# A hybrid decoder block on one core: sums of weight blocks by accumulating DMAs in the GLA value and gate projections

## The chip, the cores and the metric

The kernel runs on one core of one Trainium2 chip. The metric is the device time of one execution in microseconds. Before the change the median of three runs is 1661.94 us (1661.82 to 1663.04).

## The reference

One layer of a decoder block over 256 tokens of width 2048, float32 throughout. What matters here is the input projection and the two of its parts that the change touches, v and the output gate of the gated linear attention (GLA):

```python
proj = x @ w_in                      # x: (256, 2048), w_in: (2048, 13336)
gq, gk, gv, gr, glr, fq, fk, fv, ff, ma, mb = split(proj)
v = gv.reshape(B, S, 4, 512)         # gv: 2048 columns
o = gla_chunked(q, k, v, log_a)      # chunked linear attention, per-head RMS norm
o = o * silu(gr)                     # gr: 2048 columns, the output gate
y_gla = o @ w_branch_gla
# FoX attention -> y_fox; merged = sigmoid(ma)*y_gla + sigmoid(mb)*y_fox; merged @ w_out;
# layer norm; conv-gated MLP; layer norm; x + sigmoid(x W_g) * (p W_p)
```

## The kernel before

All weights are streamed once from DRAM, cut into units of 128 x 2048 floats that are numbered in the order of their use (`wu[u]`). A unit arrives as two tiles of 128 x 1024 (`raw`, a ring of five buffers) by DMAs on SyncE's queue, whose order is written out by hand. Each tile is split into a high part, which ScalarE rounds to the fast matmul format (`copy`, L112), and a low part, which VectorE gets as the difference (L220, L194); a product is then the three matmuls high x high, high x low, low x high. The rings `hi` and `lo` hold six tiles each. `unit(ahead=3)` prepares units up to two ahead of the one that TensorE uses. On the other engines a scheduler fixes the order of instructions when the program is built, and each engine then works in that order.

GLA's v (units 52 to 67) and gate (68 to 83) are computed in halves of 1024 output columns. The two halves of v and the first half of the gate are made by `s_half`: eight units a half, each holding one pair of 128-row blocks of the inner dimension. For a classic pair TensorE runs 24 matmuls of 512 columns. For a pair in the set `GV_S` or `GR_S` it uses a seven-product form of the 2 x 2 block product (Strassen's, in Winograd's arrangement), 21 matmuls: three of its weight operands are blocks as loaded (x11, x21, x22) and four are combinations of the four blocks b11, b12, b21, b22 of 128 x 512 (t1, t2, t3, t4). The combinations of the activations (`xS`) are made once per pair by `x_sums`. After the last seven-product pair of a half, `fold` adds the seven products up (L819), and `ev_v`, `ev_r0` (L913, L927) evacuate the half. The gate's second half is made by `x_half`, with classic units alone.

`prep_s` prepares a seven-product unit. Before, VectorE makes four differences in place in the raw tiles (`differences`, L148), two on the first tile and two on the second:

```python
if h == 0:
    sub(b11, b12, b11)
    sub(b12, b12, b22)
else:
    sub(b22, b22, b11)
    sub(b21, b21, b22)
```

The same function prepares the units of the output projection and of the down projection (u >= 120), which partly come with combinations that were parked in DRAM earlier. Seven-product units before: 53, 55, 57 (v, half 0), 61, 63, 65 (v, half 1), 69, 71 (gate, half 0).

Of the kernel before, what the change touches and what calls it, by code (L numbers as in the profile page):

```python
# [14 lines left out]
ALU = mybir.AluOpType  # L15
# [32 lines left out]
WO_ORDER = (tuple(range(8)), tuple(range(8)))  # L48
OUT_ORDER = (tuple(range(8)), (0, 1, 3, 2, 5, 4, 6, 7))
GV_S = ((1, 3, 5), (1, 3, 5))  # L50
GR_S = ((1, 3), ())
X_S = (1, 3, 5)
WO_S = ((1, 3, 5), (1, 3, 5))
WO_C = (0, 2, 4, 6, 7)
# [18 lines left out]
def tile_block(ctx: ExitStack, tc: tile.TileContext, wu, wfv, wpp, xT_in, x_in, pT_in, wlr,  # L73
               chan, gnorm, lng, ident_in, mask_in, cmask_in, out):
    nc = tc.nc
# [45 lines left out]
    for _ in range(8):  # L121
# [6 lines left out]
    s_units = {b + nh * len(order[nh]) + i  # L128
               for b, order, sset in ((52, WO_ORDER, GV_S), (68, WO_ORDER, GR_S),
                                      (120, OUT_ORDER, WO_S), (dn0, DN_ORDER, DN_S))  # L130
               for nh in range(2) for i, n in enumerate(order[nh]) if n in sset[nh]}
    ready = {}
# [34 lines left out]
    def prep_s(u):  # L167


        r0, r1 = [ring.tile([P, 1024], F32, tag="raw", bufs=5, name=f"raw{u}_{h}")  # L170
                  for h in range(2)]
        b12, b11, b22, b21 = r0[:, 0:512], r0[:, 512:1024], r1[:, 0:512], r1[:, 512:1024]
        rt = (r0, r1)
        if u in parked:
            nc.sync.dma_start(b11, wu[u, :, 512:1024])
            nc.sync.dma_start(r1, wu[u, :, 1024:2048])
            w = s8([P, 2048], name=f"td{u}")
            nc.sync.dma_start(w, td[parked[u]])
            rt = (w[:, 0:1024], w[:, 1024:2048])
        else:  # L180
            for h, r in enumerate((r0, r1)):
                nc.sync.dma_start(r, wu[u, :, h * 1024:(h + 1) * 1024])
        if dn0 <= u < dn0 + NF:
            nh = (u - dn0) // (NF // 2)
            pair = DN_ORDER[nh][(u - dn0) % (NF // 2)]
            hS[nh, pair] = s8([P, 4, 256], F32R, name=f"hS{nh}_{pair}")
            nc.sync.dma_start(hS[nh, pair].bitcast(F32), sd[DN_S[0].index(pair)].rearrange(
                "p (i n) -> p i n", i=4))

        def split(src, name, e=slice(0, 1024)):  # L190
            hi = rhi.tile([P, 1024], F32R, tag="hi", name=f"hi{u}_{name}")[:, e]
            lo = lo_tile(u, f"{u}_{name}")[:, e]
            copy(hi, src)
            nc.vector.tensor_tensor(lo, src, hi.bitcast(F32), ALU.subtract)  # L194
            return [(hi[:, o:o + 512], lo[:, o:o + 512]) for o in range(0, src.shape[1], 512)]

        x11, = split(b11, "b11", slice(512, 1024))
        x22, x21 = split(r1, "b2")
        if u not in parked:
            differences(r0, r1, 0)  # L200
        t3, t1_ = split(rt[0], "t13")
        if u not in parked:
            differences(r0, r1, 1)
        t2_, t4 = split(rt[1], "t24")
        ready[u] = [x11, x21, x22, t1_, t3, t2_, t4]
# [232 lines left out]
    for u in range(8):  # L438
        hi, lo = fvu[u]
        for j in range(2):  # L440
            kt = 2 * u + j
            a = xT[kt // 4][:, kt % 4, :]
# [6 lines left out]
            for t, i, c in seq:  # L449
                o, n = fch[c]  # L450
                w, x = prods[t][i]
# [288 lines left out]

        return o[:, i, 0:P], o[:, i, P:256]

    def s_sums(y):

        a11, a21, a12, a22 = [y[:, k, t * P:t * P + P] for k in range(2) for t in range(2)]
        v = t2("sums").rearrange("p (i t) -> p i t", t=P)
        for i, a, b, op in ((0, a21, a22, ALU.add), (2, a21, a11, ALU.subtract),
                            (1, v[:, 0], a11, ALU.subtract), (3, a12, v[:, 1], ALU.subtract)):
            nc.vector.tensor_tensor(v[:, i], a, b, op)
        return v  # L750

# [18 lines left out]
    def s_half(nm, nh, order, sset, cl, st, zof, ev, tail=0, mid={}, end=None, ahead=3,  # L770
               residual=True):

        if nh == 0:
            C = [[mmtile(f"{nm}0_{t}{c}") for c in range(2)] for t in range(2)]
            p1, p5 = [mmtile(f"{nm}0_p{i}") for i in (1, 5)]
            p6, p7 = [mxtile(f"{nm}0_p{i}") for i in (6, 7)]
        else:  # L780
            C = [[f(f"{nm}1_{t}{c}") for c in range(2)] for t, f in enumerate((mxtile, mmtile))]
            p1, p5, p6, p7 = [mmtile(f"{nm}1_p{i}") for i in (1, 5, 6, 7)]
        prods = (p1, C[0][0], C[0][1], p5, p7, p6, C[1][0])
        left = (0, 1, 6, 3, 5, 4, 2)
        n, ns = len(order), len(sset)
        todo = {id(C[t][c]): 6 * (n - ns) for t in range(2) for c in range(2)}
        for p in prods:
            todo[id(p)] = todo.get(id(p), 0) + 3 * ns
        total = dict(todo)

        def mm(ps, x, w):
            nc.tensor.matmul(ps, lhsT=x, rhs=w, start=todo[id(ps)] == total[id(ps)],  # L792
                             stop=todo[id(ps)] == 1)
            todo[id(ps)] -= 1

        def classic(pair, w, toks=(0, 1), cs=(0, 1)):
            for j in range(2):
                for t in toks:
                    ah, al = cl(pair, j, t)
                    for x, v in ((ah, w[0][j]), (ah, w[1][j]), (al, w[0][j])):  # L800
                        for c in cs:
                            mm(C[t][c], x, v[:, c * 512:c * 512 + 512])

        def strassen(pair, ops):
            for ps, i, (hi, lo) in zip(prods, left, ops):
                ah, al = st(pair, i)
                for x, v in ((ah, hi), (ah, lo), (al, hi)):
                    mm(ps, x, v)

        def fold():  # L810
            g0, g1 = 2 * nh, 2 * nh + 1
            u = t2("fold")
            axpy = lambda z, p: nc.vector.scalar_tensor_tensor(z, z, ALPHA, p, ALU.mult, ALU.add)
            add = lambda z, p: nc.vector.tensor_tensor(z, z, p, ALU.add)
            if not residual:
                copy(zof(0, g0), p1)
                for o, x, p in ((u, zof(0, g0), p6), (zof(0, g1), u, p5), (zof(1, g0), u, p7),
                                (zof(1, g1), zof(1, g0), p5)):
                    nc.vector.tensor_tensor(o, x, p, ALU.add)  # L819
                return  # L820
            copy(u, p1)
            axpy(zof(0, g0), p1)
            add(u, p6)
            axpy(zof(0, g1), u)
            add(zof(0, g1), p5)
            add(u, p7)
            axpy(zof(1, g0), u)
            add(u, p5)
            axpy(zof(1, g1), u)

        for i, pair in enumerate(order[:n - tail]):
            (strassen if pair in sset else classic)(pair, unit())
            if i in mid:
                mid[i]()
            if pair in sset and not set(order[i + 1:]) & set(sset):
                fold()
        us = [unit(ahead) for _ in range(tail)]

        def tail_mm(t, c, i):
            classic(order[n - tail + i], us[i], (t,), (c,))  # L840
            if i == tail - 1:
                ev(t, c, C[t][c])

        if tail:
            end(tail_mm)
            return
        for t in range(2):
            for c in range(2):
                ev(t, c, C[t][c])
# [4 lines left out]
    def x_sums():  # L854
        o = s8([P, 8, 256], F32R, name="xS")
        for i, pair in enumerate(X_S):
            if i < 2:
                xS[pair] = [o[:, 4 * i + j, :] for j in range(4)]
            else:
                w = [sm.tile([P, 512], F32R, tag="t2", bufs=6, name=f"xS{i}{j}") for j in range(2)]  # L860
                xS[pair] = [w[j // 2][:, j % 2 * 256:j % 2 * 256 + 256] for j in range(4)]
            y = t2("xy").rearrange("p (k t) -> p k t", t=S)
            nc.sync.dma_start(y, xT_in[:, 2 * pair:2 * pair + 2, :])
            v = s_sums(y)
            for j in range(4):
                hi = xS[pair][j][:, 0:P]
                copy(hi, v[:, j])
                nc.vector.tensor_tensor(xS[pair][j][:, P:256], v[:, j], hi.bitcast(F32),
                                        ALU.subtract)
            yield  # L870
# [53 lines left out]
    def ev_r0(t, c, ps):  # L924
        z = vg[c][:, 1, t, :]
        with tc.high_priority(P_STAT):
            nc.vector.tensor_tensor(z, z, ps, ALU.add)  # L927
        gate(z, z)

    s_half("gr", 0, WO_ORDER[0], GR_S[0], x_cl, x_st, lambda t, g: vg[g][:, 1, t, :], ev_r0,  # L930
           residual=False)
# [76 lines left out]
    for n in range(16):  # L1008
# [27 lines left out]
        i = WO_C.index(pair)  # L1036
# [242 lines left out]
    for n in range(NF):  # L1279
# [9 lines left out]
        y = t1("yc")  # L1289
# [8 lines left out]
        u = t1("up")  # L1298
# [14 lines left out]
        if pair in DN_S[0] and j == 1:  # L1313
            v = s_sums(yp)
# [199 lines left out]
def _layout(i):  # L1514
# [4 lines left out]
    for n in range(16):  # L1519
        br.append(bg[n:n + 1])  # L1520
        if n % 2 == 0:
# [5 lines left out]
        [np.stack([_wst(c("fq", 1024)), _wst(c("fk", 1024))], 1).reshape(16, P, 2048), qk.reshape(16, P, 2048), m[:PSM1],  # L1527
         _sst(c("gv", 2048), WO_ORDER, GV_S), _sst(c("gr", 2048), WO_ORDER, GR_S), m[PSM1:]] + br
        + [_sst(i["w_out"][0], OUT_ORDER, WO_S), gu,
# [45 lines left out]
```

## Time and profile before

| | |
|---|---|
| median of 3 runs | 1661.94 us (1661.82 to 1663.04) |
| span of the profiled execution, its own time | 1661.1 us |
| TensorE (PE) matmuls | 1655.3 us busy |
| VectorE (DVE) | 1278.4 us busy |
| ScalarE (ACT) | 887.5 us busy |
| GpSimd (POOL) | 61.3 us busy |
| granted TensorE clock | 1.00 |
| v and gate half 0 | 371.3 to 496.5 us of the span |

The profile records one execution, from its first to its last instruction; the runs' times also hold the little that lies around it. Matmuls are pipelined, so the length of one is more than the distance to the next. In the rows "a<-b" stands for the tile written and the tiles read, and "[0.88 <-ACT hi L112]" for idle time of the engine just before an instruction and what ended it.

### The profile page before, as it was taken

How to read it: one execution, taken by the hardware profiler on the slowest of the kernel's cores; microseconds unless marked ns; L12 is line 12 of the kernel's file. 1: busy time of each engine (PE TensorE's matmuls, PEld its weight loads, DVE VectorE, ACT ScalarE, POOL GpSimd, SP SyncE). 2: the span in 40 equal slices, each digit the busy share in tenths (PEclk: the TensorE clock that was granted, in tenths of full speed). 3: DMA queues.
4: the chain of work that ended last, by engine and by line, in shares of the span. 5: the costliest groups of instructions: out<-in, count | busy, mean ns of one | idle time of the engine just before them, and what ended most of it. 6: DMA issues, size and time to landing. Idle time of an engine off the chain costs nothing.

```text
span 1661.1 us, 24309 instructions
## 1 busy us (share of the span) xinstructions
PE 1655.3 (100%) x8935; PEld 1438.3 (87%) x8935; DVE 1278.4 (77%) x1927; ACT 887.5 (53%) x1297; POOL 61.3 (4%) x204
## 2 busy tenths in 40 slices
PE   9999999999999999999999999999999999999999
PEld 9988888888888888888898888888888888888887
DVE  7666877888876757888987777877777787898774
ACT  6655555555554654455575455555555555556543
POOL 0100000000000000000010010000000000000000
PEclk9999999999999999999999999999999999999999
DMA  8745455546564557878856587777777668798554
GB/s 321 251 164 172 169 176 171 188 158 199 196 232 172 174 181 275 309 244 301 315 171 206 207 291 266 251 243 249 254 249 255 204 226 322 275 364 316 178 188 158
DMA packets 101959, 383.74 MB, mean 231 GB/s; under 512 B 11544, under 2 KB 12832, under 8 KB 95696
## 3 DMA queue, kind: packets, MB, share of 16 engines
q1 hardware_dynamic: 97584, 359.11, 62.1%
q0 software_dynamic: 4256, 23.08, 3.7%
q8 instruction: 70, 1.15, 0.3%
q14 instruction: 49, 0.40, 0.1%
HBM read 358.02 MB, written 24.13 MB: 230 GB/s over the span
## 4 chain that ended last, share of the span: by engine, by line
PE 98%; DMA 0%; DVE 0%; ACT 0%; POOL 0%; SPq 0%; issue 0%; POOLq 0%
PE dn L792 11%; PE psu L287 9%; PE psg L287 9%; PE psm L287 7%; PE pg L333 5%; PE psu L289 5%; PE psg L289 5%; PE gv L792 4%; PE wo L792 4%; PE psm L289 4%; PE psa L287 4%; PE dn_p L792 3%; PE gr L333 3%; PE fv L452 2%; PE gr L792 2%; PE psa L289 2%
## 5 line engine op out<-in xcount | busy, mean ns | idle before, releaser
L220 DVE TENSOR_TENSOR lo<-raw,hi 128x1024 fp32r<-128x1024 f32 x502 | 611.0, 1223 | 240.4 <-ACT hi L112 238.7
L112 ACT ACTIVATE hi<-raw 128x1024 fp32r<-128x1024 f32 x502 | 528.4, 1058 | 430.5 <-issue 169.2
L287 PE MATMUL psu<-x1T,hi 128*128 128x512 f32 x688 | 240.4, 392 | 0.0
L287 PE MATMUL psg<-x1T,hi 128*128 128x512 f32 x672 | 234.8, 392 | 0.0
L289 PE MATMUL psu<-x1T,lo 128*128 128x256 f32 x688 | 192.4, 280 | 0.0
L289 PE MATMUL psg<-x1T,lo 128*128 128x256 f32 x672 | 187.9, 280 | 0.0
L287 PE MATMUL psm<-xT,hi 128*128 128x512 f32 x512 | 181.2, 396 | 0.0
L287 PEld LDWEIGHTS psu<-x1T,hi 128*128 128x128 f32 x688 | 129.2, 188 | 27.6
L287 PEld LDWEIGHTS psg<-x1T,hi 128*128 128x128 f32 x672 | 126.2, 188 | 26.9
L289 PE MATMUL psm<-xT,lo 128*128 128x256 f32 x512 | 143.2, 280 | 0.0
L289 PEld LDWEIGHTS psu<-x1T,lo 128*128 128x128 f32 x688 | 130.7, 190 | 0.0
L289 PEld LDWEIGHTS psg<-x1T,lo 128*128 128x128 f32 x672 | 127.6, 190 | 0.0
L287 PEld LDWEIGHTS psm<-xT,hi 128*128 128x128 f32 x512 | 96.2, 188 | 19.7
L792 PE MATMUL dn<-hi,hC 128*128 128x512 f32 x400 | 111.3, 389 | 0.0
L289 PEld LDWEIGHTS psm<-xT,lo 128*128 128x128 f32 x512 | 97.2, 190 | 0.1
L287 PE MATMUL psa<-oT,hi 128*128 128x512 f32 x256 | 89.5, 392 | 0.0
L792 PEld LDWEIGHTS dn<-hi,hC 128*128 128x128 f32 x400 | 75.0, 188 | 15.6
L112 ACT ACTIVATE hi_t<-raw 128x1024 fp32r<-128x1024 f32 x40 | 42.5, 1063 | 66.0 <-DVE raw L148 51.5
L112 ACT ACTIVATE hi_b<-raw 128x512 fp32r<-128x512 f32 x66 | 55.4, 842 | 40.9 <-DMA raw<-in_wu_dram 15.2
L289 PE MATMUL psa<-oT,lo 128*128 128x256 f32 x256 | 71.6, 280 | 0.0
L194 DVE TENSOR_TENSOR lo_b<-raw,hi_b 128x512 fp32r<-128x512 f32 x66 | 62.5, 954 | 9.9 <-ACT hi_b L112 9.9
L333 PE MATMUL pg<-hi,x2T 128*128 128x512 f32 (+1 forms) x256 | 69.7, 380 | 0.0
(372 smaller groups left out, 3126.3 us busy)
## 6 DMA issues: line engine op xcount, KB each, us to landing
raw<-in_wu_dram SPq DMA_DIRECT2D x555, 512.0 KB, 4.9
td<-in_wu_dram SPq DMA_DIRECT2D x13, 1024.0 KB, 8.4
td<-td POOLq DMA_DIRECT2D x13, 1024.0 KB, 6.9
td<-td SPq DMA_DIRECT2D x13, 1024.0 KB, 7.5
hS<-sd SPq DMA_DIRECT2D x19, 512.0 KB, 7.6
fvraw<-in_wfv_dram SPq DMA_DIRECT2D x13, 524.0 KB, 6.9
sd<-hs POOLq DMA_DIRECT2D x20, 256.0 KB, 5.4
lnb<-in_lng_dram SPq DMA_DIRECT2D x4, 1024.0 KB, 9.8
```

The source lines that it names most:

```text
L112: return nc.scalar.activation(o, i, AF.Copy, bias=0.0, scale=scale)
L194: nc.vector.tensor_tensor(lo, src, hi.bitcast(F32), ALU.subtract)
L220: i = nc.vector.tensor_tensor(lo, raw, hi.bitcast(F32), ALU.subtract)
L287: nc.tensor.matmul(ps, lhsT=hi[i // 8 if hoff == 0 else 0][:, w0 % 1024:w0 % 1024 + P], rhs=a[:, kt % 4, :], start=first and i == 0, stop= ...
L289: nc.tensor.matmul(ps[:, 256:512], lhsT=lo[i // 8 if hoff == 0 else 0][:, w0 % 1024:w0 % 1024 + P], rhs=a[:, kt % 4, 0:256], start=False, ...
L333: nc.tensor.matmul(bs[j][:, 0:m], lhsT=x, rhs=v[:, o:o + m], start=first and i == 0, stop=last and i == 2)
L452: nc.tensor.matmul(fbk[t][c][:, 0:n], lhsT=x, rhs=w[:, o:o + n], start=kt == 0 and i == 0, stop=kt == 15 and i == 2)
L792: nc.tensor.matmul(ps, lhsT=x, rhs=w, start=todo[id(ps)] == total[id(ps)], stop=todo[id(ps)] == 1)
```

## The change

For all units below 84 that are prepared by `prep_s`, the seven-product form is replaced by one with other signs, in which the four weight combinations are sums only: b12 + b11, (b12 + b11) + b22, b22 + b12, b21 + (b11 + b12 + b22). Two of the four (the first and the third) are made by DMAs that add a block from DRAM to a block that is already in SBUF; these are issued by GpSimd (`nc.gpsimd.dma_start(..., accum_op=ALU.add)`), 256 KB each. The other two are VectorE additions. The tiles split afterwards hold (t1, t2) and (t3, t4) instead of (t3, t1) and (t2, t4), and TensorE still takes the operands in the order x11, x21, x22, t1, t3, t2, t4. The activation sums get the matching signs in `x_sums`, the folds of these halves likewise. Pair 5 of the gate's first half (unit 73) becomes a seven-product pair. In the program's order on GpSimd the first DMAs of units 55, 63 and 71 stand ahead of the second DMAs of units 53, 61 and 69. The order of the other instructions on VectorE and ScalarE stays, except around unit 73, whose splits come before the gate's fold.

```diff
-GR_S = ((1, 3), ())
+GR_S = ((1, 3, 5), ())
@@ prep_s
+        if u < 84:
+            b12d, b11d = wu[u, :, 0:512], wu[u, :, 512:1024]
+            nc.gpsimd.dma_start(b12, b11d, accum_op=ALU.add)
+            x11, = split(b11, "b11", slice(512, 1024))
+            x22, x21 = split(r1, "b2")
+            nc.vector.tensor_tensor(b11, b12, b22, ALU.add)
+            nc.gpsimd.dma_start(b22, b12d, accum_op=ALU.add)
+            t1_, t2_ = split(r0, "t12")
+            nc.vector.tensor_tensor(b21, b21, b11, ALU.add)
+            t3, t4 = split(r1, "t34")
+            ready[u] = [x11, x21, x22, t1_, t3, t2_, t4]
+            return
@@ s_sums
-    def s_sums(y):
+    def s_sums(y, plus=False):
...
-        for i, a, b, op in ((0, a21, a22, ALU.add), (2, a21, a11, ALU.subtract),
-                            (1, v[:, 0], a11, ALU.subtract), (3, a12, v[:, 1], ALU.subtract)):
+        for i, a, b, op in (((0, a21, a22, ALU.subtract), (2, a11, a21, ALU.subtract),
+                             (1, v[:, 0], a11, ALU.subtract), (3, a12, v[:, 1], ALU.add))
+                            if plus else
+                            ((0, a21, a22, ALU.add), (2, a21, a11, ALU.subtract),
+                             (1, v[:, 0], a11, ALU.subtract), (3, a12, v[:, 1], ALU.subtract))):
@@ fold, not residual
-                for o, x, p in ((u, zof(0, g0), p6), (zof(0, g1), u, p5), (zof(1, g0), u, p7),
-                                (zof(1, g1), zof(1, g0), p5)):
-                    nc.vector.tensor_tensor(o, x, p, ALU.add)
+                for o, x, p, op in ((u, p6, zof(0, g0), ALU.add), (zof(0, g1), p5, u, ALU.subtract),
+                                    (zof(1, g0), p7, u, ALU.add),
+                                    (zof(1, g1), p5, zof(1, g0), ALU.subtract)):
+                    nc.vector.tensor_tensor(o, x, p, op)
@@ x_sums
-            v = s_sums(y)
+            v = s_sums(y, True)
```

## The prediction

> **What bounds the kernel now.** I read the page first: busy times and the chain that ended last.
>
> ```profile
> span 1661.1 us, 24309 instructions
> PE 1655.3 (100%) x8935; PEld 1438.3 (87%) x8935; DVE 1278.4 (77%) x1927; ACT 887.5 (53%) x1297; POOL 61.3 (4%) x204
> PE 98%; DMA 0%; DVE 0%; ACT 0%; POOL 0%; SPq 0%; issue 0%; POOLq 0%
> ```
>
> TensorE is busy for all but 5.8 us, and the chain is TensorE for 98%. So time can be gained only by taking matmuls away, and lost wherever an operand comes late. I then asked for the stretch of the change (value half 0, value half 1, gate half 0) and for the groups of the two output tiles.
>
> ```profile
> 371.00:497.00 126.00, 126.00 (x560) 104.39 (x559) 104.36 (x116) 66.55 (x72) 0.00 (x0) 1.00 0.63 208
> ```
> ```profile
> L792 PE MATMUL gv<-hi,xT x160: 389/389/478, 371.3 to 454.1; 128*128 128x512 f32 x160
> ```
> ```profile
> L792 PE MATMUL gr<-hi,xT x96: 389/389/390, 454.4 to 496.3; 128*128 128x512 f32 x96
> ```
>
> The first row's columns are busy us of PE, PEld, DVE, ACT and POOL (instructions in brackets), then clock, DMA share, GB/s: TensorE 126.00 of 126.00, clock 1.00, DVE 104.36 (83%), POOL nothing. The other two give the pace: between 371.3 and 454.4 stand the value's matmuls, 10 classic pairs of 24 and 6 seven-product pairs of 21, 366 in all: 83.1/366 = 0.227 us each. (The 389 ns of a row is the length of one; they overlap.) A classic pair takes 5.45 us, a seven-product pair 4.77, one of each 10.2.
>
> **What the change removes.** Pair 5 of gate half 0 (weight unit 73) goes from 24 to 21 matmuls: 3 x 0.227 = 0.7 us less on the path. Each of the nine seven-product units has two VectorE sums instead of four differences: that takes work off VectorE. TensorE waits for nothing here, so that is worth nothing by itself. The activation sums and the folds keep their number and shapes: nothing. The gate's fold moves 10.2 us later, with two classic pairs (10.9 us) behind it instead of four:
>
> ```profile
> 480.16 0.68 DVE L819 TENSOR_TENSOR vg<-vg,gr_p 128x512 f32<-128x512 f32 x1
> 496.23 2.48 DVE L927 TENSOR_TENSOR vg<-vg,gr 128x512 f32<-128x512 f32 x4
> ```
>
> It would end at about 480.8 + 10.2 = 491.0, before the evacuation at 496.2 - 0.7 = 495.5: covered by 4.5 us. Unit 73's extra splits (3.5 full-width ones instead of 2) lie in VectorE's free time.
>
> **What it adds.** Two accumulating DMAs a unit, 18 in all, 256 KB each, issued by POOL. Traffic is 4.7 MB over 126 us, 37 GB/s beside 208: no matter. What matters is the order: sum b12 += b11 (first DMA) -> VectorE add b11 = b12 + b22 -> hi/lo split of the second raw tile -> b22 += b12 (second DMA, which must wait for that split and that add, since both read b22) -> second ScalarE/VectorE split of that tile. VectorE works in program order, and in the changed program the last split still stands ahead of the next classic unit's two splits and of everything of the next seven-product unit. So a wait for the second DMA holds VectorE up. These are VectorE's rows for units 55 and 57 before:
>
> ```profile
> 378.18 1.23 DVE L220 TENSOR_TENSOR lo<-raw,hi 128x1024 fp32r<-128x1024 f32 x1 [1.49 <-ACT hi L112]
> 379.32 0.68 DVE L194 TENSOR_TENSOR lo_b<-raw,hi_b 128x512 fp32r<-128x512 f32 x1
> 380.04 0.69 DVE L148 TENSOR_TENSOR raw<-raw 128x512 f32<-128x512 f32 x1
> 380.65 1.22 DVE L194 TENSOR_TENSOR lo_b<-raw,hi_b 128x1024 fp32r<-128x1024 f32 x1
> 381.78 1.41 DVE L148 TENSOR_TENSOR raw<-raw,raw 128x512 f32<-128x512 f32 x2
> 383.23 0.69 DVE L148 TENSOR_TENSOR raw<-raw 128x512 f32<-128x512 f32 x1
> 383.84 2.52 DVE L194 TENSOR_TENSOR lo_t<-raw,hi_t 128x1024 fp32r<-128x1024 f32 x2
> 386.28 1.22 DVE L220 TENSOR_TENSOR lo<-raw,hi 128x1024 fp32r<-128x1024 f32 x1
> 388.38 1.23 DVE L220 TENSOR_TENSOR lo<-raw,hi 128x1024 fp32r<-128x1024 f32 x1 [0.88 <-ACT hi L112]
> 389.52 0.68 DVE L194 TENSOR_TENSOR lo_b<-raw,hi_b 128x512 fp32r<-128x512 f32 x1
> 394.04 2.52 DVE L194 TENSOR_TENSOR lo_t<-raw,hi_t 128x1024 fp32r<-128x1024 f32 x2
> ```
> ```profile
> 384.04 1.06 ACT L112 ACTIVATE hi_t<-raw 128x1024 fp32r<-128x1024 f32 x1 [0.39 <-DVE raw L148]
> 406.04 0.63 ACT L112 ACTIVATE hi_b<-raw 128x512 fp32r<-128x512 f32 x1 [1.62 <-DMA raw<-in_wu_dram]
> ```
>
> Before, unit 55's last split ends at 383.84 + 2.52 = 386.36 (unit 57's at 396.56), and its matmuls start at 371.3 + 69 x 0.227 = 386.9. In the new order of products the last tile (t3, t4) is met at the 5th product, not the 6th: its lo part is needed 13 matmuls in, 2.95 us after the start.
>
> **The unknown: how long an accumulating DMA takes.** The trace has none. Nearest rows, issue to landing:
>
> ```profile
> L1320 POOL DMA_DIRECT2D sd<-hs x20: 539/539/547, 895.3 to 1295.2; - x20
> DMA to landing us min/median/max: 3.8/5.4/10.8
> ```
> ```profile
> L1203 POOL DMA_DIRECT2D ppd<-ppo x4: 539/546/592, 843.3 to 848.2; - x4
> DMA to landing us min/median/max: 2.3/4.9/7.7
> ```
> ```profile
> L863 SPq DMA_DIRECT2D xy<-in_xT_dram x3: 327/402/423, 322.3 to 334.8; - x3
> DMA to landing us min/median/max: 2.8/4.0/5.9
> ```
> ```profile
> DMA to landing us min/median/max: 3.4/5.0/6.3
> ```
> ```profile
> 894.58 0.76 DVE L1318 TENSOR_TENSOR hs<-sums,hs 128x256 fp32r<-128x256 f32 x2
> 895.30 1.07 POOL L1320 DMA_DIRECT2D sd<-hs  x2 [0.47 <-DVE hs L1318]
> ```
>
> The first two are POOL's 256 KB stores, the third a 256 KB load, the fourth (the raw weight tiles from 350 to 500) the 512 KB loads of this very stretch. The floor is 2.3; the ceiling in this stretch 6.3, anywhere 10.8. An add has to read its destination too, so it moves what a 512 KB load reads: at least 3.4 when alone. POOL's median at this size is 5.4. I take the middle, 4.4 us. The last fence adds POOL's reaction: the first of two VectorE operations ends about 895.0, the DMA starts 895.30: 0.3 us.
>
> The Trainium skill (DMA: Bandwidth & Descriptors, "Anatomy of one DMA — SWDGE (gpsimd) path") prices a POOL-issued DMA at about 2.0 us plus bytes/436 GB/s, an estimate of 2.6 us for 256 KB. POOL's own rows agree at their minimum (2.3) and not at their median (5.4), which is why this is a rival below and not the forecast. Against it speaks the skill's Collectives: The Full Stack ("The bandwidth ceiling"): an inline add needs two source reads. No run here shows that yet.
>
> **The sum, at 4.4 us.** Unit 55: first split of b11 ends 380.0, add 380.7, second split 381.9, POOL at 382.2, landing 386.6, ScalarE (1.06) 387.7, VectorE (1.22) 388.9; needed 386.9 + 2.95 = 389.9: in time, by 1.0. Unit 57 (start 397.1, need 400.0): VectorE goes on from 388.9 with the classic unit's two splits (2.4) 391.3, split of b11 392.0, add 392.7, split 393.9, POOL 394.2, landing 398.6, 399.7, 400.9: 0.9 late. From there it is a loop: 2.4 + 0.68 + 0.69 + 1.22 + 0.3 + 1.06 + 1.22, less some 0.1 for operations that overlap, is 7.5 us plus the DMA: 11.9 a round against 10.2 of matmuls, 1.7 late each round. The followers 63, 65, 71 and 73 pay that: 6.8. Units 61 and 69 come behind three classic units, but the raw ring and the queues carry the delay over:
>
> ```profile
> 399.83 1.46 SPq L182 DMA_DIRECT2D raw<-in_wu_dram  x2
> 406.56 6.70 SPq L182 DMA_DIRECT2D raw<-in_wu_dram  x2
> ```
>
> The first row is unit 61's loads (the first landed just before ScalarE's 406.04, after 6.1), the second unit 63's. A load starts when a split five tiles earlier ends. Unit 57's last split at 400.9 instead of 396.56, then unit 58's two: 61's first load starts 403.2 instead of 399.83, 63's about 410.9 instead of 406.56. On POOL's queue the first DMA of 63 stands ahead of the second DMA of 61: it waits for 63's load, 410.9 + 5.7 (between the loads' median and maximum) = 416.6; then 61's DMA starts 417.2, lands 421.6, splits 423.9; needed at 418.2 + 0.9 + 2.95 = 422.0: 1.9 late. For 69 the same chain, whose turn on POOL comes about 0.9 sooner as 71's load has landed: 1.0. Sum: 0.9 + 1.9 + 1.0 + 6.8 = 10.6, less 0.7: +9.9. On the profiled span that is 1671.0; the median of the runs, 1661.94, lies 0.8 above the span, so 1671.8 us.
>
> The price moves with the landing time, one us of it being one us at each of seven or eight units. At 3.2 three followers are late by 0.3 to 0.5 and the net is +0.6 (1662.5). At 3.5 it is +3.0. At 6.3 unit 55 pays 1.2, 57 and the four followers 3.6 each, 61 and 69 4.5 each: +27.5. At 6.7 it is +31.9 (1693.8).
>
> **The rivals.**
> - Hidden (not slower). If the second DMA lands within 10.2 - 7.5 = 2.7 us, up to 3.2 with the spare time, the loop keeps pace, and only the three matmuls show: 1661.1 - 0.7 + 0.8 = 1661.2. For it: POOL's fastest store, 2.3, and a load at 2.8, and the second DMA starts while no other POOL DMA runs. Against: none of 20 stores was under 3.8, and raw loads share the engines 63% of the time. By the skill's rule of 2.6 us this is the outcome.
> - Slow adds. If adding slows the transfer itself, landing takes 7 us: units 55 to 73 pay 2.6 + 5 x 4.3 + 6.1 + 5.8 = 36 and the time is 1697. For it: POOL DMAs beside other traffic took up to 10.8. Against: this stretch has its DMA engines at 0.63.
> - Faster by more than the matmuls: VectorE's freed 2 x 0.69 us a unit would have to end a TensorE wait, and the stretch has none (126.00 of 126.00). A chance of 0.02 for what I overlook.
>
> **How the numbers follow.** 0.2% is 3.3 us, about what a measurement of this kernel can tell from no change; net +3.3 needs a landing of 3.55. Chances: hidden 0.09; landing 3.2 to 3.55 0.06; the forecast, 3.55 to 6.3, 0.68; 6.3 to 6.7 0.06; above 0.09; faster 0.02. Slower is 0.83, same 0.15. The range runs from 3.2 to 6.7, 1662.5 to 1693.8, and holds 0.80. The predicted time is the forecast's own.
>
> **What would show it.** In the changed profile: the 18 accumulating issues with a median landing near 4.4 (the number everything hangs on); a VectorE wait for ScalarE's hi_t, and that one for a DMA, of 2 to 5 us in every seven-product unit; TensorE idle before the product with t3, seven times, 0.9 to 2 us, none in unit 55; and no other stage changed. It is wrong if TensorE stays at 100% between 371 and 497 (hidden), or if the gaps stand at the first DMA's add instead, or at loads of classic units.

## The result, and the profile after

The changed kernel takes 1686.32 us (median of 4 runs, 1682.56 to 1686.61), the kernel before, run beside it, 1661.93 (1661.82 to 1663.04): a ratio of 1.014, 95% interval 1.0127 to 1.0152. It is 24.4 us slower. The forecast was 1671.8, 9.9 slower, with a range of 1662.5 to 1693.8: the sign and the place were right, the forecast loss was less than half of the measured one.

The page of the kernel after, its span, its busy times and the shares of its chain:

```profile
span 1684.7 us, 24371 instructions
PE 1663.4 (99%) x8932; PEld 1441.4 (86%) x8932; DVE 1270.0 (75%) x1915; ACT 886.4 (53%) x1299; POOL 76.9 (5%) x222
PE 91%; DMA 4%; DVE 2%; issue 2%; ACT 1%; POOL 0%; SPq 0%; POOLq 0%; ACTq 0%; DVEq 0%
```

Three matmuls fewer, VectorE 8 us less busy, and yet the chain is TensorE for 91% instead of 98%; the DMAs have 4%, which is about 67 us (4% of 1684.7) in which the chain went through a transfer. The stretch of v and gate half 0, now 25 us longer (the same window as before, with its end moved; columns as there):

```profile
371.00:522.00 151.00, 135.89 (x557) 108.05 (x556) 98.79 (x108) 67.68 (x76) 12.98 (x15) 0.95 0.68 199
```

TensorE, without a gap before, stands still for 15.1 of 151.0 us, and its mean granted clock is 0.95 where it was 1.00. Behind it nothing moved: a later stage, the 256 matmuls of `psa` with the high parts, has the same length in both traces and only starts 23.6 us later, which is the whole difference of the spans (after first, before second):

```profile
L299 PE MATMUL psa<-oT,hi x256: 391/392/393, 642.0 to 772.0; 128*128 128x512 f32 x128
```
```profile
L287 PE MATMUL psa<-oT,hi x256: 391/392/393, 618.4 to 748.4; 128*128 128x512 f32 x128
```

What TensorE waits for is in the list of waits, 355 to 520 us (who waited, for whom: us in all, times, longest). Before, only the second of these rows was in the list, with one wait of 1.5 us:

```profile
ACT hi_t L112 <- DMA raw<-in_wu_dram: 43.0, 8, 6.9
DVE lo_t L194 <- ACT hi_t L112: 38.1, 10, 6.3
PEld gv_p L807 <- ACT hi_t L112: 7.4, 4, 3.0
DVE raw L202 <- DMA raw<-in_wu_dram: 5.7, 1, 5.7
DVE raw L202 <- issue: 5.7, 1, 5.7
PEld gv_p L807 <- DVE lo_t L194: 5.0, 5, 1.1
PEld gr_p L807 <- issue: 4.1, 1, 4.1
PEld gr_p L807 <- DVE lo_t L194: 2.1, 2, 1.1
PEld gr_p L807 <- ACT hi_t L112: 1.5, 1, 1.5
```

Read it from the bottom up. TensorE's weight loads wait for the two parts of the last tile (t3, t4), VectorE's part waits for ScalarE's, and ScalarE's waits in 8 of 9 units for a DMA, up to 6.9 us. That is the loop of the prediction. The two L202 rows and the wait of 4.1 us are something else: VectorE, and TensorE behind it, waiting for the **first** DMA at the start of a half, which the forecast did not have. In VectorE's timeline that wait, at unit 61, looks so:

```profile
417.83 0.69 DVE L202 TENSOR_TENSOR raw<-raw,raw 128x512 f32<-128x512 f32 x1 [5.69 <-DMA raw<-in_wu_dram]
421.44 2.47 DVE L929 TENSOR_TENSOR vg<-vg,gv 128x512 f32<-128x512 f32 x4
425.86 1.23 DVE L194 TENSOR_TENSOR lo_t<-raw,hi_t 128x1024 fp32r<-128x1024 f32 x1 [1.95 <-ACT hi_t L112]
```

The four evacuations of the half before (L929) stand behind it in VectorE's order. At unit 69 the same happens again, at 471.82 (the profile calls that wait "issue"; the DMA issued for this sum at 464.66 landed at 471.74), and there the products need the banks that these evacuations empty; TensorE's timeline:

```profile
473.12 0.61 PE L807 MATMUL gr<-hi,xT 128*128 128x512 f32 x2
477.45 0.47 PE L807 MATMUL gr_p<-hi_b,xT 128*128 128x512 f32 x1 [3.72 <-DVE vg L929]
```

The landing times of the two DMAs, the second (L203) and the first (L199), one fence for each line:

```profile
L203 POOL DMA_DIRECT2D raw<-in_wu_dram x9: 856/862/881, 366.9 to 498.1; - x9
DMA to landing us min/median/max: 4.3/5.1/6.6
```
```profile
DMA to landing us min/median/max: 3.9/4.6/7.1
```

**The clock.** The mean of 0.95 comes from four stretches of 3.41 us at half clock. These windows of the trace are 3.41 us long; the second number after the bounds is TensorE's busy time, the third from the right the granted clock:

```profile
399.88:403.29 3.41, 1.48 (x5) 1.01 (x6) 2.25 (x2) 3.34 (x4) 0.00 (x0) 1.00 0.03 12
403.29:406.70 3.41, 3.41 (x10) 2.65 (x9) 3.41 (x4) 2.54 (x4) 0.00 (x0) 0.50 0.91 288
437.43:440.84 3.41, 0.50 (x1) 0.19 (x1) 0.91 (x1) 1.99 (x3) 0.00 (x0) 1.00 0.56 118
440.84:444.25 3.41, 3.04 (x7) 2.46 (x8) 3.38 (x5) 2.42 (x4) 0.00 (x0) 0.50 0.54 149
474.98:478.39 3.41, 0.94 (x4) 0.84 (x5) 2.92 (x5) 0.00 (x0) 0.00 (x0) 1.00 0.78 145
478.39:481.80 3.41, 3.41 (x9) 2.67 (x9) 2.29 (x3) 3.38 (x4) 0.00 (x0) 0.50 0.26 94
502.28:505.69 3.41, 1.56 (x7) 0.75 (x5) 1.31 (x2) 2.40 (x3) 0.00 (x0) 1.00 0.36 139
505.69:509.10 3.41, 3.41 (x8) 2.74 (x9) 3.41 (x4) 2.92 (x4) 0.00 (x0) 0.50 0.64 184
423.77:427.18 3.41, 2.01 (x9) 1.13 (x7) 1.46 (x3) 2.41 (x3) 0.00 (x0) 1.00 0.42 159
427.18:430.59 3.41, 3.41 (x15) 2.83 (x16) 3.38 (x4) 2.01 (x3) 0.00 (x0) 1.00 0.59 172
```

In pairs: a window in which TensorE was busy for 0.5 to 1.6 us is followed by one at clock 0.50, in which 7 to 10 matmuls are done instead of 15; the window with 2.01 is not. The stretches begin at 403.29, 440.84, 478.39 and 505.69, that is 11, 11 and 8 times 3.41 us apart: a clock of windows that runs on its own.

**Where the 24.4 us went.** Taking for every two successive weight loads the distance of their starts less the usual 0.227 us, TensorE waited in unit 55 for 0.6, 57 for 2.8, 61 for 2.1, 63 for 4.0, 65 for 2.6, 69 for 4.1, 71 for 1.0 and 73 for 2.5: 19.5 us. Some 32 matmuls at half clock took up to 0.43 us instead of 0.227: 6.2. Three matmuls fewer: -0.7. The stretch happened to start 1.0 earlier. Together 24.0, against 23.6 between the two spans.

That is TensorE's own time. The chain that ended last tells which of it counted. Before, it is TensorE's from 371 to 497 us; after, from 378 to 504 us, TensorE has 0.8% of it, about 1 us. Pieces of it (start, us, what):

```profile
404.56 6.12 DMA raw<-in_wu_dram
411.42 6.33 DMA raw<-in_wu_dram
417.83 0.67 DVE raw L202
420.25 4.41 DMA raw<-in_wu_dram
424.77 1.07 ACT hi_t L112
504.38 1.24 DVE lo_t L194
505.66 2.50 PE gr_p L807 x5
```

The first five lines are unit 61: a load, the first DMA, VectorE's sum, the second DMA, ScalarE's split. The last two are unit 73, where the chain comes back to TensorE. So the first three stretches at half clock (403.29, 440.84 and 478.39) lie beside the chain, and only the fourth lies on it.

### The profile page after: what moved, and what is told of

Same layout as the page of the kernel before. It is cut to its first block, busy times and chain, and to the rows that moved or that the text cites. A ratio compares the mean times of both kernels' runs of the same rounds, so it can differ in the third digit from the quotient of the medians.

```text
span 1684.7 us, 24371 instructions
## 1 busy us (share of the span) xinstructions
PE 1663.4 (99%) x8932; PEld 1441.4 (86%) x8932; DVE 1270.0 (75%) x1915; ACT 886.4 (53%) x1299; POOL 76.9 (5%) x222
## 4 chain that ended last, share of the span: by engine, by line
PE 91%; DMA 4%; DVE 2%; issue 2%; ACT 1%; POOL 0%; SPq 0%; POOLq 0%; ACTq 0%; DVEq 0%
PE dn L807 10%; PE psu L299 9%; PE psg L299 9%; PE psm L299 7%; PE pg L345 5%; PE psu L301 5%; PE psg L301 5%; PE wo L807 4%; PE psm L301 4%; DMA raw<-in_wu_dram 4%; PE psa L299 3%; PE dn_p L807 3%; PE gr L345 3%; PE fv L464 3%; PE psa L301 2%
## 5 line engine op out<-in xcount | busy, mean ns | idle before, releaser
L194 DVE TENSOR_TENSOR lo_t<-raw,hi_t 128x1024 fp32r<-128x1024 f32 x42 | 51.4, 1224 | 45.4 <-ACT hi_t L112 44.8
```

## The experiments

Each kernel is compared with the kernel before on the same chip, whose median there was 1662.2 to 1662.3; the difference to it is given. Diffs are against the changed kernel. Theory A is the prediction's: VectorE and ScalarE stand at the split of (t3, t4) until the second DMA has landed, with the next unit's splits behind them; its second part, formed on the trace, is that a TensorE that stands still also loses clock. The rivals are named with the runs.

**1. All four sums on VectorE, no accumulating DMA.**

```diff
-            nc.gpsimd.dma_start(b12, b11d, accum_op=ALU.add)
...
+            nc.vector.tensor_tensor(b11, b11, b12, ALU.add)
+            nc.vector.tensor_tensor(b12, b12, b22, ALU.add)
+            t3, t1_ = split(r0, "t13")
+            nc.vector.tensor_tensor(b22, b22, b11, ALU.add)
+            nc.vector.tensor_tensor(b21, b21, b22, ALU.add)
+            t2_, t4 = split(r1, "t24")
```

> All four sums are made by VectorE, no accumulating DMA; the extra pair in the gate stays. Theory A (VectorE, in program order, waits for the second DMA's landing, and TensorE for it, partly at half clock afterwards): all 19.5 us of TensorE stalls and the four half-clock stretches go, and only the three matmuls show: 0.7 us under the kernel before, 1661.2 us. Rival B (the new form itself, its products' order or the extra pair, is what costs): stays above 1670.

1661.96 us, ratio 0.9999 (0.999 to 1.0008). The window of before, in this kernel:

```profile
371.00:497.00 126.00, 126.00 (x558) 104.30 (x557) 109.90 (x124) 68.89 (x76) 0.00 (x0) 1.00 0.64 208
```

TensorE is without a gap again, though VectorE has 109.90 us of work in it, more than the 104.36 of before. The signs, the folds and the extra pair cost nothing that shows, and the three matmuls less do not show either; the accumulating DMAs are the whole loss, and the work that they take off VectorE was never worth anything.

**2. Only the first DMA.** The third sum is VectorE's.

```diff
-            nc.vector.tensor_tensor(b11, b12, b22, ALU.add)
-            nc.gpsimd.dma_start(b22, b12d, accum_op=ALU.add)
+            nc.vector.tensor_tensor(b22, b22, b12, ALU.add)
+            nc.vector.tensor_tensor(b11, b22, b11, ALU.subtract)
```

> Only the first accumulating DMA is left (b12 += b11, issued as soon as the tile has landed); VectorE makes the other three combinations. Theory A: the wait for the second DMA is gone, so 1661 to 1665 us, with at most a stall at units 61 and 69, whose first DMA is issued late. Rival C (the first DMA and its place in POOL's queue hold VectorE up): at least half of the 24 us stays, 1673 or more.

1668.23 us, ratio 1.0039 (1.0025 to 1.0053): +5.9, more than expected. Unit 73's first DMA and VectorE's wait for it, from the timelines of GpSimd and VectorE:

```profile
474.57 0.86 POOL L199 DMA_DIRECT2D raw<-in_wu_dram  x1 [15.46 <-DVE lo_t L194]
```
```profile
482.28 0.69 DVE L202 TENSOR_TENSOR raw<-raw,raw 128x512 f32<-128x512 f32 x1 [2.89 <-DMA raw<-in_wu_dram]
```

Issued at 474.57, it landed 7.6 us later, the longest of nine (median 4.9), and VectorE's add started at 482.28, while SyncE's queue had loads of raw tiles back to back from 474.36 on. So the first DMA is not free either: where it meets a run of loads it lands late enough to hold up VectorE.

**3. Only the second DMA.**

```diff
-            nc.gpsimd.dma_start(b12, b11d, accum_op=ALU.add)
             x11, = split(b11, "b11", slice(512, 1024))
+            nc.vector.tensor_tensor(b12, b12, b11, ALU.add)
```

> Only the second accumulating DMA is left (b22 += b12, after the add and the split); VectorE makes b12 + b11. Theory A: the steady stall of 2 to 3 us a unit stays; only the 4.1 us at unit 69, where the evacuation stands behind the wait for the first DMA, shrinks: 1679 to 1686 us. Rival C: back to 1661 to 1665.

1676.18 us, ratio 1.0084 (1.007 to 1.0098): +13.9, less than expected. The second DMA is the larger part, but +13.9 and +5.9 do not make up the +24.4 that both cost together.

**4. Without the extra pair.**

```diff
-GR_S = ((1, 3, 5), ())
+GR_S = ((1, 3), ())
```

> Both DMAs, but pair 5 of the gate's first half (unit 73) stays classic. Theory A: one stall of 2.5 us and one half-clock stretch of 1.7 us fewer, three matmuls (0.7) more: 1682 to 1684 us. Rival D (the extra pair is what costs, by the late fold or the held buffers): about 1662.

1681.82 us, ratio 1.0116 (1.01 to 1.0131): +19.5, at the lower edge of Theory A's band and far above Rival D's. Units 53 to 71 lose almost as much as in the changed kernel; the pair in unit 73 adds some 5 us of waiting for the 0.7 us that it saves.

**5. Plain copies instead of accumulating.** This leaves out two of the four sums.

```diff
-            nc.gpsimd.dma_start(b12, b11d, accum_op=ALU.add)
+            nc.gpsimd.dma_start(b12, b11d)
-            nc.gpsimd.dma_start(b22, b12d, accum_op=ALU.add)
+            nc.gpsimd.dma_start(b22, b12d)
```

> Leaves out two of the four weight sums: both of GpSimd's DMAs copy their block over the destination instead of adding to it; issue order, queue, size and waits stay. Theory A (the loop VectorE - GpSimd's second DMA - ScalarE - VectorE; the second DMA landed in 5.1 us in the median, the first in 4.6): if it is the adding that takes the time, a plain copy lands nearer the 256 KB load's 2.8 to 4.0 us, the loop of 7.5 us + landing falls to 10.3 to 11.5 against 10.2, and the time to 1662 to 1672 us. Rival F (a 256 KB transfer issued by GpSimd among this stretch's 512 KB loads lands in about 5 us whatever it does): landing stays at 4.6 and 5.1, time 1682 to 1688.

1673.7 us, ratio 1.0067 (1.005 to 1.0084): +11.5, just above Theory A's band, far below Rival F's. The second DMA's rows:

```profile
L203 POOL DMA_DIRECT2D raw<-in_wu_dram x9: 536/536/538, 367.3 to 488.2; - x9
DMA to landing us min/median/max: 3.6/4.0/5.0
```

A plain copy of the same 256 KB lands in 4.0 us instead of 5.1 (the first one in 3.7 instead of 4.6), and its issue keeps GpSimd busy for 536 ns instead of 862. So about 1 us of the landing goes with the adding, the longer issue included; the other 4 us are what a plain copy takes here, and they alone cost 11.5.

**6. The late split.** Both DMAs stay; the split of (t3, t4) is put behind the two splits of the next classic unit, on ScalarE and VectorE.

```diff
-            t3, t4 = split(r1, "t34")
-            ready[u] = [x11, x21, x22, t1_, t3, t2_, t4]
+            def rest():
+                t3, t4 = split(r1, "t34")
+                ready[u] = [x11, x21, x22, t1_, t3, t2_, t4]
+            pending.append(rest)
...
```

What is in `pending` is run at the end of the next unit's `prep`.

> Both DMAs stay; only the split of the last tile (t3, t4) is put behind the two splits of the following classic unit on ScalarE and VectorE. Theory A (what costs is that VectorE and ScalarE stand at that split, with the classic unit's splits queued behind it): the loop loses the classic unit's 2.4 us and is about 5.2 us + 5.1 of landing = 10.3 against 10.2, so the waits of the followers (57, 63, 65, 71, 73) go from 2 to 3 us to under 0.5 each; what the first DMA costs at the starts of the halves stays, as it did alone (+6): 1664 to 1671 us. Rival H (the late landing itself, or the queue, holds TensorE up, wherever the split stands): the split is also later now, 1684 to 1695.

1674.45 us, ratio 1.0075 (1.006 to 1.009): +12.2, half of the loss gone, 3.5 us short of what was expected. The same two rows of the list of waits as above:

```profile
ACT hi_t L112 <- DMA raw<-in_wu_dram: 16.1, 6, 3.6
DVE lo_t L194 <- ACT hi_t L112: 12.8, 9, 2.4
```

43.0 and 38.1 us have become 16.1 and 12.8. The second DMA itself is not much shorter (4.7 in the median instead of 5.1), but less is queued behind the wait for it. The first DMA has got worse (median 6.9 instead of 4.6), which is where the missing 3.5 us are to be looked for.

**7. The late split, with the second DMA only** (the edits of experiments 3 and 6 together).

> Only the second DMA (the first sum is VectorE's), and the split of (t3, t4) behind the following classic unit's splits. Theory A: without the first DMA and with the loop at 10.3 to 10.5 against 10.2, hardly anything is left of the 14 us that the second DMA cost alone: 1661 to 1665. Rival H: no less than the second DMA alone, 1676 and more.

1662.35 us, ratio 0.9999 (0.999 to 1.0009). Experiment 3's 13.9 us are gone to within the measurement, by an order of instructions alone:

```profile
371.00:497.00 126.00, 126.00 (x554) 103.53 (x554) 103.10 (x115) 67.89 (x75) 6.91 (x8) 1.00 0.74 226
```

Nine accumulating DMAs of 4.2 us in the median run in this stretch, and TensorE has no gap. That is Theory A's sharpest point, and it held: what the second DMA cost was not the transfer's length by itself but the classic unit's splits behind the wait for it.

**8. VectorE makes the first sum in units 61 and 69**, on top of the late split (first) and in the changed kernel alone (second).

```diff
+            if u not in (61, 69):
                 nc.gpsimd.dma_start(b12, b11d, accum_op=ALU.add)
             x11, = split(b11, "b11", slice(512, 1024))
+            if u in (61, 69):
+                nc.vector.tensor_tensor(b12, b12, b11, ALU.add)
```

> The kernel with the late split, and in units 61 and 69, which open their halves, the first sum is VectorE's instead of a DMA's. Theory I (at those two the first DMA, issued behind back-to-back loads, landed after 6 to 8 us, and VectorE's add and the evacuations of the half before stood behind it): the waits of 2.0 and 1.9 us at 61 and 69 go and those that follow shrink: 1666 to 1671 us. Rival J (what is left of the late split's 12 us comes from the loop of the followers, whose landing is 4.7 to 5.7): 1672.5 to 1676.

> The changed kernel with nothing else done but that: in units 61 and 69 the first sum is VectorE's. Theory I: unit 69's wait of 4.1 us for a free bank, its stretch at half clock (1.6 us) and most of 61's 2.1 us go, the followers keep their 2 to 3 us each: 1675 to 1680. Rival J: 1683 to 1687.

On top of the late split: 1668.2 us, ratio 1.0039 (1.0026 to 1.0052), +6.0, a gain of 6 us as Theory I said. In the changed kernel: 1683.87 us, ratio 1.0129 (1.0114 to 1.0144), +21.6, as Rival J said. Both hold, each in its kernel. In the second one the wait of 4.1 us for the banks at unit 69 is gone from the list, but TensorE now waits longer for t3 of unit 61: 3.4 us, the longest such wait of a weight load, where the longest in the changed kernel is 3.0:

```profile
PEld gv_p L810 <- ACT hi_t L112: 6.2, 3, 3.4
```

The wait comes back through GpSimd's queue. VectorE had everything ready for unit 61's second DMA at 414.55, but in GpSimd's order the first DMA of unit 63 stands ahead of it, and that went only at 417.28; the second followed at 417.93 and landed 6.4 us later. At unit 69 it was ready at 464.81 and went at 467.75.

**9. Zero matmuls in the waits**, to keep TensorE from standing still: 10 before the product with t3 in all nine units (first), 8 in units 57, 63, 65 and 73 (second), 58 in all where the changed kernel's trace has its waits (third). They have an all-zero weight block and add nothing. The first kernel's edit, in the loop over the products:

```diff
+                for _ in range(FILL):
+                    nc.tensor.matmul(C[0][1], lhsT=zero, rhs=ops[2][0], start=False, stop=False)
```

> Ten matmuls with an all-zero weight block stand before the product with t3 in each of the nine seven-product units, into a bank that is being summed up, so the result is the same: TensorE works through 2.3 us of its wait instead of standing still. Theory A's second part (the four stretches of 3.41 us at half clock, 6.2 us lost, come from TensorE standing still for 2.5 us and more): the stretches that follow waits of t3 go, only unit 69's wait for its banks stays, and the time is 1678 to 1683 us, since the loop of VectorE and the DMA, not TensorE's work, sets the pace. Rival G (the half clock has nothing to do with the standing still): 32 matmuls stay at half rate and the extra 2.3 us of units 53 and 55, which hardly waited, come on top: 1686 to 1692.

> Eight matmuls with an all-zero weight block (1.8 us; they add nothing to the result) before the product with t3 in units 57, 63, 65 and 73 alone, whose waits there were 2.8, 2.9, 2.6 and 2.5 us. Theory A's second part (TensorE loses half its clock for a stretch of 3.41 us after a stretch of 3.41 us of which it stood still for over 2.1 to 2.3 us): three of the four stretches go, the one after unit 69's wait may stay, the zero matmuls lie inside the waits: 1680 to 1683.5 us and at most one or two stretches. Rival G (the stretches do not depend on the standing still): four stretches, 1685 to 1688.

> The changed kernel with 58 matmuls with an all-zero weight block, 13.2 us, put where TensorE waited in its trace: before the product with t3 of units 57, 61, 63, 65 and 73 (6 to 10 each) and before the first product of units 61 and 69 (6 and 11); they add nothing to the result. No single wait should then be over 2 us. It tells whether the stretches at half clock cost time of their own. Theory A's second part, additive: no stretch or one, and the 6 us are won back, 1679 to 1682. Rival K (the stretches come from the standing still, but the time lost in them would be spent waiting for VectorE and the DMA anyway): no stretch or one, and 1683 to 1687. Rival G (no link): three or four stretches, 1684 to 1690.

1699.88 us (+37.7), 1684.72 (+22.5) and 1695.59 (+33.4): none within its own theory's band, and the first and the third above every band. The first put 20.4 us of work into 19.5 us of waits, at places of which some hardly waited. The second was absorbed: 7.3 us of matmuls more, and no longer than the changed kernel. Its windows:

```profile
424.43:427.84 3.41, 1.67 (x6) 0.86 (x5) 1.60 (x2) 2.69 (x3) 0.00 (x0) 1.00 0.86 225
427.84:431.25 3.41, 3.41 (x9) 2.63 (x8) 3.38 (x5) 1.74 (x4) 0.00 (x0) 0.50 0.72 204
472.21:475.62 3.41, 0.00 (x0) 0.00 (x0) 3.41 (x6) 0.00 (x0) 1.77 (x2) 1.00 0.58 65
475.62:479.03 3.41, 3.31 (x8) 2.67 (x9) 0.89 (x2) 1.43 (x2) 0.00 (x0) 0.50 0.81 196
```

Units 57 and 63, whose waits were filled, no longer have a stretch at half clock behind them; units 61 and 69, which were not filled, have one (69 follows a window without a single matmul), and unit 73, which still waited 3.4 us, too. That speaks for the link with standing still and against Rival G, but it does not tell what the stretches cost. The third kernel shows why such filling is no clean test. There, GpSimd's queue at unit 73's first DMA (L201) and unit 71's second (L205), and ScalarE's split behind the latter:

```profile
491.86 0.87 POOL L201 DMA_DIRECT2D raw<-in_wu_dram  x1 [13.93 <-DMA raw<-in_wu_dram]
492.44 1.18 POOL L205 DMA_DIRECT2D raw<-in_wu_dram  x1
```
```profile
498.60 1.06 ACT L114 ACTIVATE hi_t<-raw 128x1024 fp32r<-128x1024 f32 x1 [10.27 <-DMA raw<-in_wu_dram]
```

In this kernel the order on GpSimd's queue puts unit 73's first DMA ahead of unit 71's second, which in the changed kernel goes first. The second was ready at about 488.3, when VectorE's split of the tile ended, and stood until 492.44 behind the first, which waited for a load; ScalarE waited 10.3 us for it.

## Why the prediction was wrong in its size

**Right.** The kernel before is bound by TensorE; the new form, unit 73's splits and the later fold cost nothing that shows, and VectorE's freed time is worth nothing (experiment 1, 0.3 us under the kernel before, within the measurement; so the gain of 0.7 is not shown either). The larger part of the loss comes from VectorE's order around the second DMA (experiments 3, 6, 7). Of the signs named, the waits of ScalarE for the DMA and of VectorE for ScalarE are there, nothing outside this stretch moved, and TensorE waits before the product with t3 in seven units, though for 0.6 to 4.0 us instead of 0.9 to 2; unit 55, forecast at 0, is one of them, and unit 69 waits for its banks instead.

**Term 1, the landing time, was mis-sized where it counts.** The prediction took 4.4 us, the middle between 3.4 for a 512 KB load and 5.4 for GpSimd's stores, for every accumulating DMA. The median of all 18 was 4.7, not far from it. But the loop goes through the second DMAs of the units 57, 63, 65, 71 and 73, and these landed after 5.5, 6.6, 6.6, 4.7 and 5.1 us, 5.7 in the mean; the second DMAs of 53, 61 and 69 took 4.3 to 4.4. The loop itself was right. From the start of one split of (t3, t4) to the next, VectorE took 12.9, 14.1, 14.1, 12.3 and 12.6 us in these five rounds, each time the prediction's 7.5 plus that round's own landing time, to 0.1 us. Forecast were 11.9 a round, so the five together were 6.4 us longer. Why the landings differ so much is not shown.

The argument behind the 3.4, that an add moves what a load of twice the size reads, was not bad in kind: the second DMA took 1.1 us more in the median than the plain copy (experiment 5). But the plain copy's 4.0 was already above that floor. The Trainium skill's rule (DMA: Bandwidth & Descriptors, "Anatomy of one DMA — SWDGE (gpsimd) path"), an estimate of 2.6 us for this size, is too short for these DMAs, which ran among loads: no one of the 18 took under 3.9, and even the plain copies took 3.2 and more. That an inline add needs two source reads, as the Trainium skill has it (Collectives: The Full Stack, "The bandwidth ceiling"), agrees with the 1.1 us in its direction.

**Term 2, the first DMA, was costed at nothing for VectorE, and it is not nothing.** The step that made unit 61 late by 1.9 and unit 69 by 1.0 had the lateness of the half starts come from GpSimd's queue, where 63's first DMA waits for its load and lets 61's second go only at 417.2. 63's first DMA was indeed issued as late as 417.63. But in this kernel it held nothing up: unit 61's own first sum was there only at 417.8, because the DMA for it, issued at 411.42 among loads, took 6.3 us. VectorE stood for that 5.7 us, at unit 69 again, and the evacuations of the half before behind it. Unit 61's 2.1 was thus right by its size and wrong by its cause, which is luck; unit 69's 4.1 was four times the forecast. The queue that the forecast named stood behind this: where VectorE makes the first sum, unit 61's second DMA does wait on GpSimd for 63's first, until 417.9 (experiment 8, second kernel). Alone the first DMA costs 5.9 (experiment 2); of the 12.2 that are left with the late split, 6.3 go with it at the half starts and another 5.8 with the rest of it (experiments 6, 8, 7).

**Term 3, the clock, was not in the sum at all.** The prediction treated a wait of TensorE as costing its own length. The trace has 6.2 us more, spent in matmuls at half rate behind such waits, but by the chain only the fourth stretch counts, with some 1.6 us. In the other three the matmuls at half rate take the place of waiting. TensorE came to the product with t3 in unit 63 at 439.95 and in unit 65 at 454.04, 14.1 us apart, which is VectorE's round between them, though 1.4 us of it went into the half clock; its wait in unit 65 was the shorter for that. This is read from one trace, and no run here takes the half clock away alone: the zero matmuls did not settle it. In the late split two executions with a mean clock of 1.000 took 1672.71 and 1673.29 us and two with 0.998 took 1675.61 and 1676.81, but an execution that happens to wait longer would show both.

**Together**, 6.4 us for the five rounds, 3.1 for unit 69 and 1.6 for the clock are 11.1 of the 13.7 us that the span grew beyond the forecast's 9.9. The rest lies in unit 55 and in the way from 57 to 61, which took 24.8 us from split to split where the forecast has 23.0 (an estimate from its own times).

In the sums that give the range, unit 55 is wrong by a little: by the forecast's own times it pays 0.9 and not 1.2 at a landing of 6.3, and 1.6 and not 2.6 at 7. The forecast at 4.4 doesn't hang on it.

**The rivals.** "Hidden" at 1661.2 did not come true here, but experiment 7 is that case for the second DMA, by another order and not by a faster landing. "Slow adds" took the right direction; its 7 us was reached only as the maximum of the first DMAs (7.1). "The gaps stand at the first DMA's add instead", named as a sign of error, was half true: they stand at both.

The changes, in one line each, make up the loss: 24.4 us with both DMAs; 12.2 with the late split; 6.0 with VectorE's first sum at the half starts as well; 0.1 without any first DMA. No kernel here beats the one before by more than the measurement can tell: what could be won were three matmuls.

## What to carry to other kernels

Before an operation is given to a DMA, write down the loop that it enters: the time from issue to use, and everything that stands behind that use in the order of each engine that waits; nine transfers, with medians of 4.2 and 4.5 us, were free when the waiting instruction stood last and cost 14 us when a unit's work was queued behind it. Price a transfer by the trace's rows at their upper half when it runs among loads, and give every new DMA such a price, not only the one on the obvious path. A median over all transfers is not the price in the loop: here it was 4.7 where the loop's own took 5.7. And where a TensorE that never stood still begins to wait, look at its granted clock too, and at the chain that ended last, which tells whether the lost clock counted.

## What the runs showed of the hardware

- **A half clock comes after partial idleness, on a window of its own.** In this stretch TensorE's granted clock went from 1.00 to 0.50 for 3.41 us, or for two such windows on end, in nine of the kernels measured. In the window of 3.41 us just before such a stretch TensorE was busy for 0.0 to 1.77 us; no window of this stretch with 1.80 us or more had that consequence. In between it isn't sharp: in experiment 4 a window with 1.48 us busy was followed by full clock, the next, with 1.25, by half:

```profile
469.54:472.95 3.41, 1.48 (x7) 0.90 (x5) 3.38 (x4) 1.06 (x1) 1.75 (x2) 1.00 0.39 60
472.96:476.37 3.41, 1.25 (x6) 1.07 (x7) 2.61 (x5) 0.00 (x0) 0.00 (x0) 1.00 0.80 170
476.37:479.78 3.41, 3.41 (x10) 2.67 (x9) 2.12 (x2) 3.21 (x4) 0.00 (x0) 0.50 0.19 77
```

  The Trainium skill (TensorE: Matmul & The Clock Gate, Part 1) has the free-running window and the half rate, and the traces agree with it: 3.41 us, 0.50. It asks for an idle window; the traces show that a window about half idle can do it (1.48 and 1.56 us busy, in the changed kernel). So it matters where a wait falls: in experiment 4 TensorE waited 3.4 us at unit 61 across two windows, busy for 1.67 and 2.14 us, and the clock stayed at 1.00.
- **An accumulating DMA of 256 KB, DRAM to SBUF, issued by GpSimd, took 3.9 to 7.1 us** in the changed kernel (up to 8.1 in the others); the plain copy of the same size 3.2 to 6.5. Its issue kept GpSimd busy for 0.86 us instead of 0.54.
